# Retention gates and the last two heads' values as a second seven-product block product

## The chip, the cores and the metric

One core of a Trainium2 chip runs the whole program. Its engines work side by side: TensorE (PE in the profile, with its weight loads as PEld), VectorE (DVE), ScalarE (ACT), GpSimd (POOL) and the queues that issue transfers (SP for plain loads, POOL for loads that add to what is already there). The metric is device time in microseconds (us) of one execution, as the median of several runs.

## The reference

A trunk of two layers over 512 tokens of width 1024, in float32. Cut to what matters here:

```python
y = rms_norm(h, mix_norm[i])
proj = y @ w_in[i]                     # [512, 1024] @ [1024, 6144]
x_lru, g_lru, q, k, v, g_ret, u_sgu, v_sgu, g_sgu = jnp.split(proj, split_points, axis=-1)
lru_out = rg_lru(causal_depthwise_conv(x_lru, ...), ...)
ret_out = retention(q, k, v, positions, ret_norm[i])   # 6 heads of 128, chunks of 128 tokens
sgu_out = spatial_gating(u_sgu, v_sgu, ...)
mixed = jnp.concatenate([lru_out * silu(g_lru), ret_out * silu(g_ret), sgu_out * silu(g_sgu)], -1)
h = h + mixed @ w_out[i]
z = rms_norm(h, ple_norm[i])
h = h + sigmoid(z @ w_ple_gate[i]) * (p[i] @ w_ple_proj[i])
```

In retention a head's output rows `o` (per token) are normalised, `o * rsqrt(mean(o*o) + EPS) * g_norm`, and then multiplied by the gate. The widths are 768 for q, k, v and g_ret (6 heads of 128) and 512 for v_sgu.

## The kernel before, in words

Activations lie as feature rows: a tile has 128 features on the partitions and 512 tokens along them. Every float32 operand of a large product is split in a high and a low part, and a product takes three matmuls, high·high, high·low, low·high (`mm3`, lines 212 to 216). A feature step (`feat_steps`) makes 128 output features for all 512 tokens: 8 blocks of the inner dimension times 3 matmuls of 512 columns, 24 in all.

Weights come in chunks of 128 x 1024 (`plan`, the list of all chunks in the order of use). `emit_raw` loads a chunk, `emit_cv` splits it: ACT casts it to `whi` (line 165) and DVE subtracts to get `wlo` (line 170). For a few chunks (`xl` features 3 to 5, without the first layer's feature 3) ACT writes the negated cast and POOL's queue adds the stored weights to it (lines 167 and 168). `prefetch` runs `LOOK` = 4 chunks ahead of use; `whi`, `wlo` and `raw` have four buffers each.

V of the SGU and the values of heads 0 to 3 are token rows (tokens on the partitions), 512 columns each. They are made by a block product with seven multiplications in place of eight (`FAST`, Strassen's scheme in Winograd's form): the tokens, the inner dimension and the columns are halved, four operands on the token side are sums (`fast_sums`, tiles `uy`), and the weight-side sums are made by the load itself, by adding stored quarter blocks in the tile `rawq` (`W11`, then `Ta`, `Tc`, `Td` each on top of the last) or in `raw` (`Tb`, two blocks). Each of the seven steps (`fast_step`) takes two chunks and 2 x 4 x 3 = 24 matmuls of 512 columns. Lines 609 to 623 add the products up in `v4` and `vs`. The values of heads 4 and 5 come from `tok_steps`, two steps of 48 matmuls of 256 columns ahead of head 4. The gate of a head is a feature step (`gr`), scaled by the norm row `R` and put through Silu on ACT (`silu_scaled`).

The order of a layer: six conv-channel steps `xl`, the seven products, layer norm (`ln_apply`), then SGU steps (`gs`, `u`) with the LRU groups (`lru_group`, four groups of two blocks of 96) between them, SGU's output product (`sgu_out`), the six heads, six LRU gate steps `gl`, the output products `oret` and `olru`, and the gated embedding. A head has the feature steps k, q and gr; then its small matmuls hang between later steps by a countdown: `side.extend([[1, scores], [2, states], [3, omm], [5, otr]])`, where `step` counts down by one behind its matmuls. `scores` takes transposes and products of k and q, `states` the chunk states, `omm` the outputs with their mean square and rsqrt, `otr` the transposes back to feature rows and the product with the gate, which is then split (`split_to`) for `oret`. k, q, rope's halves (`rt`) and the square of the outputs (`oq`) lie in tiles with one buffer each, `rt` and `oq` in the same one (`qt`). Background work waits in two lists (`bg`, three items a step, and `lazy`, one a step), such as the splits of the LRU operands (`lru_split`, tiles `xc`), the gates' tanh, exp and sqrt, and the rope tables.

The program order sets only the priority. A planner puts the instructions on the engines in its own order of readiness, so an instruction can run long before its place in the text if its inputs and buffers are there.

Of the kernel before, what the change touches and what calls it, by code (L numbers as in the profile page):

```python
# [30 lines left out]
FIRST = ("W11", "W21", "Ta")  # L31
RSQRT_MAGIC = 1597463007.0
# [35 lines left out]
def blocks_of(chunk):  # L68

    l, kind, idx, n = chunk  # L70
    if kind != "fast":
        return [chunk]
    return [(l, "quad", (q, idx[1]), n) for q in {"Ta": ("W12",), "Tc": ("W22",), "Tb": ("W12", "W22"), "Td": ("W21",)}.get(idx[0], idx[:1])]
# [6 lines left out]
def rows(chunk):  # L80
# [4 lines left out]
SLOTS = [  # L85
    {"y": range(0, 16), "uy": range(16, 32), "v": range(36, 40), "vs": range(32, 36), "xc": range(16, 20), "sgu": range(22, 30), "v45": (30, 31),
     "ret": list(range(22, 30)) + list(range(32, 36)), "lru": list(range(36, 40)) + list(range(16, 22)) + [30, 31], "p": range(32, 36)},
    {"y": range(16, 32), "uy": range(0, 16), "v": range(36, 40), "vs": range(32, 36), "xc": range(0, 4), "sgu": range(6, 14), "v45": (14, 15),
     "ret": list(range(6, 14)) + list(range(32, 36)), "lru": list(range(36, 40)) + list(range(0, 6)) + [14, 15], "p": range(0, 4)},
    {"y": range(0, 0)},  # L90
]
# [3 lines left out]
def trunk(ctx, tc, a):  # L95
# [30 lines left out]
    def after(i):  # L126

        l, kind, idx, n = chunks[i]
        before = {"Ta": "W11", "Tc": "Ta", "Td": "Tc"}.get(idx[0]) if kind == "fast" else None
        return chunks.index((l, kind, (before, idx[1]), n)) if before else -1  # L130

    def emit_raw():
# [18 lines left out]
    def emit_cv():  # L151
# [9 lines left out]
        else:  # L161
# [4 lines left out]
            if kind == "in" and 3 * P <= idx < OFF["gl"] and i > 3:  # L166
# [63 lines left out]
    first3 = [wp.tile([P, 1024], F32, tag="raw", name=f"raw{i}") for i in range(3)]  # L230
# [75 lines left out]
    def norm_stat(t0=0, nt=4, diag=True):  # L306
# [21 lines left out]
        nrm["dg"] = [tp.tile([P, S], F32R, tag=t, name="n" + t, bufs=b) for t, b in (("sgm", 1), ("sq", 2))]  # L328
# [17 lines left out]
    def feat_steps(l, y, kinds, evicts, look=LOOK, n_bg=3, mid=None, n_lazy=1, tag=()):  # L346
# [3 lines left out]
        def pe():  # L350
# [3 lines left out]
            for k in range(KD):  # L354
                for acc, (wh, wl) in zip(accs, ws):
# [5 lines left out]

    def tok_steps(l, y, off, evict):

        ws = []
        for th in range(2):
            accs = []

            def pe():
                if not ws:
                    ws.extend([take(l, "inv", (off, 0)), take(l, "inv", (off, 1))])  # L370
                acc = bank(shape=(P, 2, 256))
                accs.append(acc)
                for j in range(2):
                    t = slice(P * (2 * th + j), P * (2 * th + j) + P)
                    for k in range(KD):
                        wh, wl = ws[k // 4]
                        c = slice(256 * (k % 4), 256 * (k % 4) + 256)
                        mm3(acc[:, j, :], y[k][0][:, t], y[k][1][:, t], wh[:, c], wl[:, c], k == 0, k == KD - 1)

            step(pe, lambda: evict(th, accs[0]), look=LOOK if th == 0 else LOOK - 2)  # L380
# [25 lines left out]
    def rope_tables():  # L406
        ang, n1, n2, tmp = slot_tiles((20, 21, 30, 31), "rope")
# [20 lines left out]
        def last():  # L428
            V.tensor_scalar(ang, ang, float(np.float32(3.1415925)), -float(np.float32(3.1415925)), op0=ALU.min, op1=ALU.max)
            SC.activation(sinT, ang, AF.Sin, scale=inv[:, 1:2])  # L430
            SC.activation(n1, ang, AF.Abs)
            SC.activation(cosT, n1, AF.Sin, scale=-1.0, bias=cst[:, 0:1])

        ops = [first, rnd(n1, big), red(n1, c1[0]), red(n1, c1[1])]
        ops += [red(n1, c1[2], out=tmp), red(n1, c1[3], out=tmp, x=tmp), rnd(n2, 2 * np.pi, x=tmp), red(n2, c2[0])]
# [51 lines left out]
    for l in range(DEPTH):  # L487
# [101 lines left out]
        banks = {}  # L589

        def fast_step(name, xn, at):

            first = name in FIRST

            def pe():
                ws = [take(l, "fast", (name, c)) for c in range(2)]
# [9 lines left out]
            def ev():  # L606
                for t in range(2):
                    acc = banks[at][t]
                    if name == "W11":
                        SC.copy(v4[t], acc)  # L610
                    elif name == "W21":
                        V.tensor_add(v4[t], acc, v4[t])
                    elif name == "Tc":
                        SC.copy(vs[t], acc)
                    elif name == "Tb":
                        SC.copy(vs[2 + t], acc)
                        V.tensor_sub(vs[2 + t], banks["Y"][t], vs[2 + t])
                        ln_stats(2 + t)
                    elif name == "W22":
                        V.tensor_sub(vs[t], acc, vs[t])  # L620
                        ln_stats(t)
                    elif name == "Td":
                        SC.copy(v4[2 + t], acc)
# [78 lines left out]
        for product in FAST:  # L702
            fast_step(*product)
        ln_apply()
# [352 lines left out]
```

## Time and profile before

| | |
|---|---|
| median of 3 runs | 924.42 us (923.02 to 926.29) |
| profiled execution, its own time | 922.63 us |
| its span, first to last instruction | 920.9 us |
| mean granted TensorE clock | 0.995 |
| PE matmuls busy | 900.2 us, 4354 instructions |
| DVE busy | 663.6 us, 1284 instructions |
| ACT busy | 459.8 us, 665 instructions |
| POOL busy | 48.8 us, 49 instructions |

Busy time of PE is modelled from pipelined matmuls: a matmul shows 0.39 us although the next one starts sooner, so the rate is read from the distance of two starts. A row of the stage view lists, after the stretch and its length, busy time and (instructions) of PE, PEld, DVE, ACT and POOL, the granted clock, the share of the transfer engines and GB/s; instructions that only touch the edge of a stretch are counted in it. A row of the timeline has start and length in us, engine, line, operation, tile written <- tiles read, and in brackets the idle time before and what ended it.

### The profile page before, as it was taken

The page shows a single profiled execution, that of the slowest core. Times are in us where ns is not written, and L with a number is a line of the kernel's source. Part 1 is how long each engine was busy: PE and PEld are TensorE (multiplying, and loading weights), DVE is VectorE, ACT ScalarE, POOL GpSimd, SP SyncE. Part 2 cuts the span into 40 slices and gives each one's busy share as a digit, 9 for nine tenths or more (in the row PEclk, how much of TensorE's full clock was granted, in tenths as well). Part 3 has the DMA queues.
Part 4 walks back from the last instruction along what each step waited for, and adds up shares of the span by engine and source line. Part 5 has one row for each costly group of instructions (what it writes and reads, how often), then busy time and mean ns, then how long its engine had stood idle before and what let it go on. Part 6 is the DMA issues. An engine that isn't in the chain of part 4 may idle for free.

```text
span 920.9 us, 11714 instructions
## 1 busy us (share of the span) xinstructions
PE 900.2 (98%) x4354; PEld 752.0 (82%) x4354; DVE 663.6 (72%) x1284; ACT 459.8 (50%) x665; POOL 48.8 (5%) x49
## 2 busy tenths in 40 slices
PE   9999998999999999999998999899999999999997
PEld 7788786788898888888887888688889888888886
DVE  7899997978766764448737998788776676534564
ACT  6655769823332433335537556976233334334353
POOL 0210000000000000200211000000000000011020
PEclk9999999999999999999999999999999999999999
DMA  8976222332222332331257852132221223333302
GB/s 298 247 177 224 59 92 70 115 115 75 87 69 98 99 109 95 126 137 69 92 128 147 215 164 75 52 125 97 77 92 69 95 82 109 88 106 128 102 1 92
DMA packets 34745, 103.57 MB, mean 112 GB/s; under 512 B 4608, under 2 KB 5632, under 8 KB 34688
## 3 DMA queue, kind: packets, MB, share of 16 engines
q1 hardware_dynamic: 27680, 85.42, 27.8%
q0 software_dynamic: 3024, 11.01, 6.5%
q10 hardware_dynamic: 3984, 6.38, 2.4%
q8 instruction: 34, 0.56, 0.2%
q14 instruction: 23, 0.19, 0.1%
HBM read 94.41 MB, written 2.10 MB: 105 GB/s over the span
## 4 chain that ended last, share of the span: by engine, by line
PE 82%; DVE 9%; DMA 3%; issue 3%; ACT 2%; SPq 0%; DVEq 0%; POOL 0%; ACTq 0%; POOLq 0%
PE acc L216 24%; PE acc L215 24%; PE acc L214 24%; DVE wlo L170 2%; DMA rawq<-in_wall 1%; PE sc L826 1%; PE o L849 1%; DMA wlo<-in_wall 1%; PE o L851 1%; PE kv L837 1%; PE pp L214 1%; DVE xcv L551 1%; PE pp L216 1%; PE pp L215 1%; DVE rope L415 1%
## 5 line engine op out<-in xcount | busy, mean ns | idle before, releaser
L165 ACT CAST whi<-raw 128x1024 fp32r<-128x1024 f32 (+2 forms) x157 | 153.1, 978 | 306.4 <-PE acc L215 217.0
L216 PE MATMUL acc<-y,wlo 128*128 128x512 f32 x608 | 238.9, 393 | 4.6 <-DMA wlo<-in_wall 4.6
L214 PE MATMUL acc<-y,whi 128*128 128x512 f32 x608 | 242.6, 399 | 0.3 <-DVE whi L470 0.2
L215 PE MATMUL acc<-y,whi 128*128 128x512 f32 x608 | 238.1, 392 | 0.0
L170 DVE TENSOR_TENSOR wlo<-raw,whi 128x1024 fp32r<-128x1024 f32 (+2 forms) x152 | 171.2, 1129 | 75.5 <-ACT whi L165 75.4
L216 PEld LDWEIGHTS acc<-y,wlo 128*128 128x128 f32 x608 | 114.5, 188 | 29.9 <-DMA wlo<-in_wall 5.5
L214 PEld LDWEIGHTS acc<-y,whi 128*128 128x128 f32 x608 | 115.0, 189 | 24.0 <-ACT rg L663 0.6
L215 PEld LDWEIGHTS acc<-y,whi 128*128 128x128 f32 x608 | 114.9, 189 | 22.9 <-DVE y L284 0.4
L304 POOL TENSOR_TENSOR nacc<-nacc,sq 128x512 f32<-128x512 f32 (+1 forms) x21 | 28.6, 1360 | 497.4 <-ACT sq L294 497.4
L214 PE MATMUL acc<-z,whi 128*128 128x512 f32 (+1 forms) x144 | 53.0, 368 | 0.0
L216 PE MATMUL acc<-z,wlo 128*128 128x512 f32 (+1 forms) x144 | 52.8, 367 | 0.0
L215 PE MATMUL acc<-z,whi 128*128 128x512 f32 (+1 forms) x144 | 52.8, 367 | 0.0
L216 PE MATMUL acc<-ml,wlo 128*128 128x512 f32 x96 | 37.4, 390 | 0.0
L215 PE MATMUL acc<-rm,whi 128*128 128x512 f32 x96 | 37.4, 390 | 0.0
L214 PE MATMUL acc<-ml,whi 128*128 128x512 f32 x96 | 37.4, 390 | 0.0
L215 PE MATMUL acc<-ml,whi 128*128 128x512 f32 x96 | 37.4, 390 | 0.0
L214 PE MATMUL acc<-rm,whi 128*128 128x512 f32 x96 | 37.4, 390 | 0.0
L216 PE MATMUL acc<-rm,wlo 128*128 128x512 f32 x96 | 37.4, 390 | 0.0
L214 PE MATMUL acc<-whi,y 128*128 128x256 f32 (+1 forms) x112 | 37.2, 332 | 0.0
L215 PE MATMUL acc<-wlo,y 128*128 128x256 f32 (+1 forms) x112 | 36.9, 329 | 0.0
L216 PE MATMUL acc<-whi,y 128*128 128x256 f32 (+1 forms) x112 | 36.8, 329 | 0.0
L914 DVE TENSOR_TENSOR hT<-hT,acc 128x512 f32<-128x512 f32 x16 | 11.0, 687 | 29.9 <-PE acc L216 29.9
(233 smaller groups left out, 1651.9 us busy)
## 6 DMA issues: line engine op xcount, KB each, us to landing
raw<-in_wall SPq DMA_DIRECT2D x119, 512.0 KB, 3.4
raw<-in_wall SPq DMA_DIRECT2D x32, 384.0 KB, 3.0
rawq<-in_wall POOLq DMA_DIRECT2D x12, 512.0 KB, 6.5
wlo<-in_wall POOLq DMA_DIRECT2D x5, 512.0 KB, 9.0
hT<-in_xT SPq DMA_DIRECT2D x8, 256.0 KB, 5.9
rawq<-in_wall SPq DMA_DIRECT2D x4, 512.0 KB, 6.2
raw<-in_wall POOLq DMA_DIRECT2D x4, 512.0 KB, 9.7
out_dram<-o SPq DMA_DIRECT2D x8, 256.0 KB, 2.1
```

The source lines that it names most:

```text
L165: SC.copy(hi[:m, :n], r[:m, :n])
L170: V.tensor_sub(lo[:m, :n], r[:m, :n], f32(hi[:m, :n]))
L214: T.matmul(out, wh, xh, start=first, stop=False, skip_group_check=more)
L215: T.matmul(out, wh, xl, start=False, stop=False, skip_group_check=more)
L216: T.matmul(out, wl, xh, start=False, stop=last, skip_group_check=more)
L304: (V if d == KD - 1 else e).tensor_add(nrm["acc"][:, c], nrm["acc"][:, c], sq[:, :n])
L415: return lambda: V.scalar_tensor_tensor(out, n, -c, x, op0=ALU.mult, op1=ALU.add)
L551: V.scalar_tensor_tensor(u[:, j:], xs[:, : S - j], col(V_CW, l * 24 + 6 * (3 - j) + c), u[:, j:], op0=ALU.mult, op1=ALU.add)
L826: T.matmul(b[:, n, :], k[:, c], q[:, c], start=True, stop=True)
L837: T.matmul(kv[:, n, :], hd["kn"][:, n, :], values(h, n), start=True, stop=True)
L849: T.matmul(o[:, c], hd["s"][:, n, :], values(h, n), start=True, stop=n == 0)
L914: V.tensor_add(hT[:, d, :], hT[:, d, :], accs[j])
```

## The change

The gates of all six heads (768 columns) and the values of heads 4 and 5 (256 columns) become a second block product of seven steps on the same token sums, with 2 x 512 columns. Its results are token rows `d1` and `d2`, so the gate is multiplied into the normalised output rows before the transposes back. The `gr` steps and `tok_steps` go. A head has two feature steps; the countdown of the small matmuls runs in half steps. The split of q and k weights takes the road by ACT and POOL, that of `xl` the one by DVE. `raw` has three buffers in place of four; the LRU operands use the tile `rawq`; `lru_split` moves ahead in the background list; layer norm runs behind the first of the new products; some slots and tags move.

```diff
+FAST_COLS = (((OFF["v"], 512),), ((OFF["vs"], 512),)), (((OFF["gr"], 512),), ((OFF["gr"] + 512, 256), (OFF["v"] + 512, 256)))
...
-        out += [(l, "fast", (name, c), 1024) for name, _, _ in FAST for c in range(2)]
+        out += [(l, "fast", (name, c, g), 1024) for g in range(2) for name, _, _ in FAST for c in range(2)]
...
-            if h == 4:
-                out += [(l, "inv", (OFF["v"] + P * h, kh), 1024) for kh in range(2)]
-            out += [(l, "in", OFF[n] + P * h, 1024) for n in ("k", "q", "gr")]
+            out += [(l, "in", OFF[n] + P * h, 1024) for n in ("k", "q")]
...
+        "d1": [40, 41, *at(12, 13)], "d2": at(4, 5, 8, 9), "sgu": at(2, 3, 6, 7, 10, 11, 14, 15),
...
-            r = wp.tile([P, 1024], F32, tag="raw", name=f"raw{i}")
+            r = wp.tile([P, 1024], F32, tag="raw", name=f"raw{i}", bufs=3)
...
-            if kind == "in" and 3 * P <= idx < OFF["gl"] and i > 3:
+            if kind == "in" and OFF["q"] <= idx < OFF["v"]:
...
-    def step(pe, evict=None, look=LOOK, n_bg=3, pre=None, n_lazy=1):
-        prefetch(st["use"] + look)
-        pe()
+    passed = []
+
+    def half_step():
+
+        passed.append(1)
         for e in side:
             e[0] -= 1
         while side and side[0][0] <= 0:
             side.pop(0)[1]()
+
+    def step(pe, evict=None, look=LOOK, n_bg=3, pre=None, n_lazy=1):
+        prefetch(st["use"] + look)
+        passed.clear()
+        pe()
+        half_step()
+        if not passed[1:]:
+            half_step()
...
             for k in range(KD):
+                if k == KD // 2 and len(kinds) == 1:
+                    half_step()
...
-                for b, x in zip(LRU_GROUPS[g], act_tiles(SLOTS[l]["xc"], f"xc{l}{g}_")):
+                for b in LRU_GROUPS[g]:
+                    t = wp.tile([P, 2 * S], F32R, tag="rawq", name=f"xc{b}", bufs=2)
+                    x = t[:, :S], t[:, S:]
...
-        def fast_step(name, xn, at):
+        def fast_step(g, name, xn, at):
 
             first = name in FIRST
+            r1, r2 = ((v4, vs), (d1, d2))[g]
...
-            fast_step(*product)
-        ln_apply()
+            fast_step(0, *product)
+        bg.append(ln_apply)
+        for product in FAST:
+            fast_step(1, *product)
+        drain()
+
+        def gates(t):
+
+            def f():
+                for x in (d1[t], d2[t][:, :256]):
+                    SC.activation(x, x, AF.Silu, scale=rn[:, t : t + 1])
+
+            return f
+
+        bg.extend([gates(t) for t in range(4)])
...
-                bg.append(lru_split(c - 1))
+                (bg.append if c == 2 else bg.appendleft)(lru_split(c - 1))
...
-                    bg.append(lru_split(3))
+                    bg.appendleft(lru_split(3))
...
-            if h == 4:
-                v45 = slot_tiles(SLOTS[l]["v45"], f"v45{l}_")
-                tok_steps(l, y, OFF["v"] + P * h, lambda th, acc: SC.copy(v45[th].rearrange("p (a b) -> p a b", a=2), acc))
...
-                    SC.activation(ob[:, P * t : P * t + P], o[:, P * t : P * t + P], AF.Copy, scale=r[:, t : t + 1])
+                    c = slice(P * t, P * t + P)
+                    V.scalar_tensor_tensor(ob[:, c], o[:, c], r[:, t : t + 1], gate(h, t), op0=ALU.mult, op1=ALU.mult)
...
-                oT = bank("o", 1, name="oT")
+                oT = bank(name="oT")
...
-                V.scalar_tensor_tensor(m, oT, col(V_RN, l * 6 + h), hd["sg"], op0=ALU.mult, op1=ALU.mult)
-                split_to(rm[h], m)
-
-            feat_steps(l, y, [("in", OFF["gr"] + P * h)], [g_ev])
-            side.extend([[1, scores], [2, states], [3, omm], [5, otr]])
+                w = col(V_RN, l * 6 + h)
+                SC.activation(rm[h][0], oT, AF.Copy, scale=w)
+                V.scalar_tensor_tensor(rm[h][1], oT, w, f32(rm[h][0]), op0=ALU.mult, op1=ALU.subtract)
+
+            side.extend([[2, scores], [3, states], [4, omm], [7, otr]])
```

## Rows read from the trace of the kernel before

**Rows 1.** The page's first part: busy us, share of the span, instructions.
```profile
PE 900.2 (98%) x4354; PEld 752.0 (82%) x4354; DVE 663.6 (72%) x1284; ACT 459.8 (50%) x665; POOL 48.8 (5%) x49
```

**Rows 2.** Stage view: layer 0's SGU, single stretches, a retention head.
```profile
30.59:45.49 14.90, 12.79 (x49) 10.09 (x48) 12.74 (x28) 10.20 (x17) 4.04 (x5) 0.89 1.04 222
482.35:496.02 13.67, 11.19 (x50) 8.94 (x48) 8.83 (x22) 7.56 (x13) 2.42 (x3) 1.00 1.06 223
133.53:148.86 15.33, 12.50 (x50) 9.38 (x49) 15.21 (x22) 15.21 (x20) 0.00 (x0) 0.89 0.14 46
583.28:597.74 14.46, 11.44 (x50) 8.12 (x49) 13.77 (x20) 13.65 (x17) 0.00 (x0) 1.00 0.13 46
248.36:254.19 5.83, 5.83 (x52) 5.83 (x51) 4.64 (x16) 0.70 (x2) 0.00 (x0) 1.00 0.27 90
214.40:234.72 20.32, 20.32 (x110) 17.33 (x109) 15.96 (x40) 6.75 (x14) 0.00 (x0) 1.00 0.23 79
...
96.00:142.00 46.00, 42.22 (x201) 34.26 (x199) 45.55 (x78) 35.75 (x46) 0.00 (x0) 1.00 0.22 69
142.00:172.00 30.00, 29.82 (x123) 23.37 (x124) 24.60 (x34) 26.66 (x35) 0.00 (x0) 0.94 0.22 73
```

**Rows 3.** PE's waits: line waited for, us in total, times, longest.
```profile
PE acc L214 <- ACT xc L495: 5.1, 2, 2.8
PE acc L216 <- DMA wlo<-in_wall: 4.6, 2, 2.5
...
PE mx L716 <- DVE vs L636: 1.0, 1, 1.0
```

**Rows 4.** Timeline of PE in a feature step, twelve matmuls apart.
```profile
180.41 0.39 PE L214 MATMUL acc<-y,whi 128*128 128x512 f32 x1
...
183.13 0.39 PE L214 MATMUL acc<-y,whi 128*128 128x512 f32 x1
```

**Rows 5.** Groups by line: count | busy us, mean ns | idle before.
```profile
L165 ACT CAST whi<-raw 128x1024 fp32r<-128x1024 f32 (+2 forms) x157 | 153.1, 978 | 306.4 <-PE acc L215 217.0 <-issue 68.2 <-PE acc L216 16.4
...
L170 DVE TENSOR_TENSOR wlo<-rawq,whi 128x1024 fp32r<-128x1024 f32 x16 | 19.5, 1221 | 1.9 <-ACT whi L165 1.8
...
L830 DVE SCALAR_TENSOR_TENSOR s<-sc,kf,mask 128x128 f32<-128x128 f32 x48 | 13.5, 345 | 1.4 <-PE sc L826 1.2
...
L167 ACT ACTIVATE wlo<-raw 128x1024 fp32r<-128x1024 f32 x5 | 5.3, 1052 | 0.0
```

**Rows 6.** Landing of `rawq` loads at 499 and at 30 us; the page's plain loads.
```profile
DMA to landing us min/median/max: 5.1/5.3/7.7
...
DMA to landing us min/median/max: 7.3/7.8/8.3
...
raw<-in_wall SPq DMA_DIRECT2D x119, 512.0 KB, 3.4
```

**Rows 7.** Timeline of DVE, and one row of PE, around a head's outputs.
```profile
220.16 0.69 DVE L798 TENSOR_TENSOR rtq<-acc,sinT 64x512 f32<-64x512 f32 x1 [0.85 <-PE acc L216]
...
228.00 0.48 PE L214 MATMUL acc<-y,whi 128*128 128x512 f32 x1
...
228.76 0.68 DVE L800 TENSOR_TENSOR q<-acc,cosT 128x512 f32<-128x512 f32 x1
...
230.91 0.69 DVE L858 TENSOR_REDUCE ov<-oq 128x4 f32<-128x512 f32 x1 [0.75 <-ACT oq L856]
...
234.02 0.16 DVE L862 TENSOR_TENSOR rs_y<-rs_y,of 128x4 f32<-128x4 f32 x1
```

**Rows 8.** Timelines of DVE and POOL at 30 and at 480 us.
```profile
30.63 1.39 DVE L854 TENSOR_TENSOR of<-of 128x4 f32<-128x4 f32 x1
...
31.03 0.96 POOL L577 TENSOR_SCALAR_AFFINE_SELECT ws<-ws 128x512 f32<-128x512 f32 x1
...
480.64 1.22 DVE L170 TENSOR_TENSOR wlo<-rawq,whi 128x1024 fp32r<-128x1024 f32 x1
...
480.65 0.87 POOL L145 DMA_DIRECT2D raw<-in_wall  x1 [1.49 <-DMA raw<-in_wall]
```

More of the change, by code (lines that the diff above doesn't have):

```diff
@@ L72, in blocks_of @@
         return [chunk]
-    return [(l, "quad", (q, idx[1]), n) for q in {"Ta": ("W12",), "Tc": ("W22",), "Tb": ("W12", "W22"), "Td": ("W21",)}.get(idx[0], idx[:1])]
+    return [(l, "quad", (q, *idx[1:]), n) for q in {"Ta": ("W12",), "Tc": ("W22",), "Tb": ("W12", "W22"), "Td": ("W21",)}.get(idx[0], idx[:1])]
 def stored():
@@ L81, in rows, with slots, at @@
     return LB if chunk[1] == "lg" else P
[L85 to L91, printed above, removed]
+def slots(y0, z0):
+    def at(*offs):
+        return [z0 + o for o in offs]
+    return {
+        "y": range(y0, y0 + 16), "uy": range(z0, z0 + 16), "vs": range(32, 36), "v": range(36, 40),
+        "d1": [40, 41, *at(12, 13)], "d2": at(4, 5, 8, 9), "sgu": at(2, 3, 6, 7, 10, 11, 14, 15),
+        "ret": [*at(2, 3, 6, 7, 10, 11, 14, 15), *range(32, 36)],
+        "lru": [*at(0, 1), *range(36, 40), *at(12, 13, 4, 5, 8, 9)], "p": [40, 41, 42, 32],
+    }
+SLOTS = [slots(0, 16), slots(16, 0), {"y": range(0, 0)}]
 @with_exitstack
@@ L129, in after @@
         before = {"Ta": "W11", "Tc": "Ta", "Td": "Tc"}.get(idx[0]) if kind == "fast" else None
-        return chunks.index((l, kind, (before, idx[1]), n)) if before else -1
+        return chunks.index((l, kind, (before, *idx[1:]), n)) if before else -1
     def emit_raw():
@@ L228, in trunk @@
     hT = cp.tile([P, KD, S], F32, name="hT")
-    first3 = [wp.tile([P, 1024], F32, tag="raw", name=f"raw{i}") for i in range(3)]
+    first3 = [wp.tile([P, 1024], F32, tag="raw", name=f"raw{i}", bufs=3) for i in range(3)]
     half = [slice(0, 512), slice(512, 1024)]
@@ L327, in norm_stat @@
         V.tensor_sub(rl, r, f32(rh))
-        nrm["dg"] = [tp.tile([P, S], F32R, tag=t, name="n" + t, bufs=b) for t, b in (("sgm", 1), ("sq", 2))]
+        nrm["dg"] = [tp.tile([P, S], F32R, tag=t, name="n" + t, bufs=b) for t, b in (("m2", 2), ("sq", 2))]
         for x, dg in zip((rh, rl), nrm["dg"]):
@@ L360, in feat_steps @@
         step(pe, lambda: [e(acc) for e, acc in zip(evicts, accs)], look=look, n_bg=n_bg, n_lazy=n_lazy)
[L362 to L380, printed above, removed]
     def split_to(x, src, e=None):
@@ L406, in rope_tables @@
     def rope_tables():
-        ang, n1, n2, tmp = slot_tiles((20, 21, 30, 31), "rope")
+        (ang,), n1, n2 = slot_tiles((42,), "ang"), cosT, sinT
         big = 2 * np.pi * 2.0**14
@@ L589, in trunk @@
         banks = {}
-        def fast_step(name, xn, at):
+        d1 = slot_tiles(SLOTS[l]["d1"], f"d1{l}_")
+        d2 = slot_tiles(SLOTS[l]["d2"], f"d2{l}_")
+        def fast_step(g, name, xn, at):
             first = name in FIRST
+            r1, r2 = ((v4, vs), (d1, d2))[g]
             def pe():
-                ws = [take(l, "fast", (name, c)) for c in range(2)]
+                ws = [take(l, "fast", (name, c, g)) for c in range(2)]
                 if first:
@@ L783, in values, with gate @@
         def values(h, n):
-            if h < 4:
-                return v4[n][:, P * h : P * h + P]
-            return v45[n // 2].rearrange("p (a b) -> p a b", a=2)[:, n % 2, P * (h % 2) : P * (h % 2) + P]
+            return v4[n][:, P * h : P * h + P] if h < 4 else d2[n][:, P * h - 256 : P * h - 128]
+        def gate(h, n):
+            return d1[n][:, P * h : P * h + P] if h < 4 else d2[n][:, P * h - 512 : P * h - 384]
         for h in range(NH):
-            if h == 4:
-                v45 = slot_tiles(SLOTS[l]["v45"], f"v45{l}_")
-                tok_steps(l, y, OFF["v"] + P * h, lambda th, acc: SC.copy(v45[th].rearrange("p (a b) -> p a b", a=2), acc))
+            hd = {}
             hd = {}
@@ L994, in layout @@
         if kind == "quad":
[L995 to L996 removed]
+            k, cols = int(idx[0][1]) - 1, FAST_COLS[idx[2]][int(idx[0][2]) - 1]
+            x = np.stack([np.concatenate([w_in[l][P * j : P * j + P, f0 : f0 + nf] for f0, nf in cols], 1) for j in (4 * idx[1] + k, 4 * idx[1] + 2 + k)], 1)
         elif kind == "p":
```

31 lines of the change are left out of this document (12 added, 19 removed).

## The prediction

> **What bounds the kernel now.** I read the page's engine lines first [rows 1]: PE is busy nearly all of the span. A busy PE only counts if it is at its rate, so I read the spacing next [rows 4]: twelve matmuls apart, two starts of 512 columns lie 2.72 us apart, 0.2267 us each; the granted clock of such stretches is 1.00, the 2.4 GHz level (the head in [rows 2]). A step of 24 matmuls is 24 × 0.2267 = 5.44 us. Where PE keeps this spacing it is the bound, and only its matmul count and its waits set the time. So I looked for stretches with the count right and the time too long [rows 2, 3]. There are three kinds. The two conv-channel steps `xl4`, `xl5` take 14.90 us in layer 0 and 13.67 in layer 1 for 48 matmuls (10.88): 4.0 and 2.8 us lost, to `wlo` from the accumulating DMA [rows 3]; in layer 0 the clock's mean fell to 0.89 there. The last SGU gate step, LRU group 2 and the first SGU output matmuls (24 + 12 + 10 = 46 matmuls, 10.43 us) take 15.33 and 14.46: 4.9 and 4.0 us lost, behind the LRU operand copies `xc` of ACT [rows 3]. And 1.0 us goes to the layer norm's `vs`. In the retention heads nothing is lost: a head's cycle of 20.32 us is PE throughout, DVE 15.96 [rows 2]. DVE is the second bound in layer 0's SGU stage, with 45.55 of 46 us, and LRU groups 2 and 3 are hard on ACT (26.66 of 30).
>
> **The change part by part.**
>
> *Matmuls.* Twelve `gr` feature steps go: 12 × 5.44 = 65.3 us. The four half-steps of `tok_steps` go: one half is 48 matmuls of 256 columns in 5.83 us [rows 2], four are 23.3 us. Fourteen product steps come, each 2 × 4 × 3 = 24 matmuls of 512 columns like the products there now: 14 × 5.44 = 76.2 us. Sum: **-12.4 us**. All three lie on PE, at its rate, so this part is as sure as the spacing.
>
> *Weight splits.* `gr` and `v45` had 16 chunks in all, the second product has 28. A chunk costs ACT a cast of 0.98 us and DVE a subtraction of 1.22 [rows 5]. The 24 `k` and `q` chunks leave DVE for a second ACT pass of 1.05 us and an accumulating DMA on POOL. In retention that takes three subtractions (3.66 us) and two 512-column operations (the R multiply and one of the split, 2 × 0.69, priced by the 0.68 of the q multiply [rows 7]) off DVE, and adds four gate multiplies of 128 columns at 0.345 [rows 5], 1.38: 15.96 - 3.66 - 1.38 + 1.38 = 12.3 us of DVE per head, under PE's 20.32 - 5.44 - 0.1 = 14.8. The second product needs 14 × 1.22 + 6 × 0.68 = 21.2 us of DVE in 38.1 us of PE, so DVE gets some 17 us there in which rope tables and layer norm can run that now crowd the SGU stage. The eight gate activations per layer sit on ACT, 35.75 of 46 us busy there [rows 2]; each is shorter than the cast of 0.98, so at most 7.8 of the 10.2 us free. All this costs nothing while PE covers it. It loads 16 blocks of 512 KB a layer, 8.4 MB in 38 us or 220 GB/s, which is the rate of the crowded stretch at 30.59 (222, the transfer engines' share 1.04); hence the crowded landing times below.
>
> *The `xl` chunks go back to DVE.* The wait for their DMA goes, at most 6.8 us. But DVE then has two more subtractions: in layer 0, 12.74 + 2.4 = 15.1 us of work where PE will need only 10.88, so it is 4 us behind and the next thing late is `Ta`, whose sums and weight split DVE makes. I keep 1.0 of the 4.0. In layer 1 it has 8.83 + 2.4 = 11.2 against 10.88, about even; I keep 1.9 of the 2.8. **-2.9 us** (0 to -6.8).
>
> *Layer norm a product earlier:* the wait on `vs` goes, **-1.0** (0 to -1.0).
>
> *`lru_split` to the front of the background list.* Now the copies for group 2 stand behind tanh, exp and sqrt of group 1; ACT is busy 15.21 of 15.33 us there, so the order decides. Ahead of them, the copy is ready a whole gate step (5.44) before PE asks. Of 8.9 us I take **-5.0**, near the middle between all (-8.9) and the little (-2) that is left if the sigmoids then come late, since ACT's work is the same and PSUM waits on it.
>
> *New waits.* The sums in `rawq` are a chain: split, accumulate, split. Let t = 0 be the start of the first product's last step, where `W11` of the second gets weight buffers (four pairs, two per step). Cast 1.05, subtraction 1.22, landing 5.3 alone or 7.8 crowded [rows 6], cast, subtraction: 9.8 to 12.3 us; `Ta` needs it at two steps, 10.88. So up to 1.5 us late, 4 with DVE two subtractions behind too. I take 0.8 a layer, **+1.6** (0 to +8). `raw` with three buffers: the second `Tb` chunk must wait for a `W21` chunk's split, then load (3.4), accumulate, split: 1.05 + 1.22 + 3.4 + 5.3 to 7.8 + 2.27 = 13.2 to 15.7 us of the 16.3 that three steps leave; **+0.5** for four places (0 to +4). The first `k` chunk: 2 × 1.05 + 5.3 to 7.8 = 7.4 to 9.9 us, against two output steps and LRU group 3 (13.6); ACT is 26.66 of 30 busy and may start it late: **+0.5** (0 to +3). Behind each such wait PE's queue stands still; DVE and ACT catch up.
>
> *The heads' chain.* Scores now come one step after q instead of two, and states and outputs half a step apart. Count from the end of a head's outputs, the earliest at which q may be overwritten (one buffer). Now: the step behind the outputs starts at 228.00; the q multiply starts at 228.76, the square's sum at 230.91, the rsqrt chain ends at 234.2 [rows 7]. With one more operation of 0.7 q is done 2.2 us after the outputs, and it is needed after a k step, 5.44: 3 us of cover. The normalised rows are ready after 6.2 plus four gate multiplies, 7.6; the transposes stand behind 36 matmuls of 512 columns at least, 8.2. So PE stays the bound, on the second count by little; I take 0.1 a head for handovers, **+1.2** (0, since nothing is lost now, to +29, below).
>
> *POOL.* 24 + 16 - 5 = 35 accumulating DMAs more, 0.87 us each on an idle engine [rows 8]. Does POOL disturb DVE? Once it does: an `of` multiply of four columns, 0.16 elsewhere [rows 7], takes 1.39 beside POOL's mask of `ws`, and both end within 0.03 us of each other. But beside a DMA issue the weight subtraction keeps its 1.22. The Trainium skill, page "SBUF — State Buffer", section "Who interferes with whom", says that the two share a port pair as an exclusive lock, by which the loser of a collision stands still for the other's whole instruction, and that DVE in two-port modes can starve descriptor generation. The first pair of rows agrees with a lock; the second shows none for a DMA issue beside this subtraction. By the row the 24 issues in the heads cost nothing.
>
> *Sum:* -12.4 - 2.9 - 1.0 - 5.0 + 1.6 + 0.5 + 0.5 + 1.2 = **-17.5 us**. The profiled execution took 922.63 (span 920.9 and 1.7 around it), so 905.1; the median of the runs shown is 1.8 above it, so I state 924.4 - 17.5 = 906.9, **907 us**.
>
> **The rivals.**
>
> *Waits move into the second product.* `Ta` and `Tb` are late at their upper ends (+12 instead of +2.1): 917. For it: the crowded landing and DVE's fullness in layer 0. Against: the later links of the same chain lose nearly nothing in the first product, and DVE has slack in the second.
>
> *ACT stays the bound at the LRU groups*, so that 2 of the 8.9 come back, and nothing of the 6.8: 907 + 3.0 + 2.9 = 913. For it: ACT full there, and gate and `k` passes added. Against: the lost time is one late copy, not the sum of ACT's work.
>
> *The heads become a DVE latency chain: slower.* `qt` is one buffer for rope's halves and for the square of the outputs. If in DVE's order the norm chain takes it first, q's rope starts after the gate multiplies: 0.8 for the square, 3.3 from its sum to the rsqrt (230.91 to 234.2), 1.4, and then four operations, 2.7: 8.2 us, where scores want it at 5.44 and the transposes of k, some tenths. That is about 2.4 us a head, +29 in all and -1.2 for what the sum has there: 935. It decides from 17.5 / 12 = 1.5 us a head. For it: the outputs now come in the step of q itself. Against: the planner orders by readiness (the `of` multiply of a head's outputs runs at 30.63, in layer 0's first steps [rows 8]), and q's halves are ready a block of outputs before the square; the half at 220.16 ran as soon as its step's last matmul released it [rows 7].
>
> *A port lock between POOL and DVE in the heads.* Two issues of 0.87 a head stop DVE: 12.3 + 1.7 = 14.0 of 14.8 us. By the sum PE still covers it; my estimate is half a microsecond a head lost to order, 913. The page named above would have it so for two-port operations; the second pair of rows 8 speaks against.
>
> **How the numbers follow.** My forecast 0.62; waits in the second product 0.18; ACT 0.06; the heads' chain 0.10; the lock 0.04. Less than 0.3% (2.8 us, about what the three runs' spread of 3.3 allows) is no change. All cases but the third end faster, with some of the second's tail near no change; the heads' chain at half its price is no change too. Faster 0.86, same 0.05, slower 0.09. Low end: the matmuls and all three recoveries without any new wait, -12.4 - 6.8 - 1.0 - 8.9 = -29.1, would be 895; 896 leaves hardly anything out. High end: the second product's and ACT's cases together give 923; 921 leaves about one in ten above, the heads' case.
>
> **What would show it.** PE with 4354 - 288 - 192 + 336 = 4210 matmuls; a head's cycle of 14.8 us; no wait of PE on the accumulated `wlo` in the `xl` steps; DVE not full in the second product; `xc` no longer ended by ACT at group 2. Wrong would be: PE gaps at the second `Ta` or at `Tb` above 2 us, a cycle above 16 us with PE waiting for q, or the 46 matmuls around LRU group 2 still at 14 us.

## The result and the profile after

The changed kernel takes 931.56 us (median of 4 runs, 930.40 to 932.75), the kernel before 925.05 beside it (4 runs, 923.02 to 926.29): ratio 1.0076, 95% interval 1.0057 to 1.0095, so slower by 6.5 us where 17.5 faster was forecast. The profiled execution of the changed kernel took 930.40 (span 928.5).

The page's first part (busy us, share of the span, instructions of each engine), to be read beside [rows 1]:

```profile
PE 894.8 (96%) x4210; PEld 739.4 (80%) x4210; DVE 654.5 (70%) x1313; ACT 482.4 (52%) x662; POOL 79.6 (9%) x84
```

The 4210 matmuls are there, and PE's busy time fell by 5.4 us; but the span grew by 7.6, so PE now stands still for longer. PE's waits (line waited for, us in total, times, longest), to be read beside [rows 3]:

```profile
PE acc L230 <- ACT vs L619: 7.8, 2, 5.7
PE acc L230 <- ACT xc L495: 4.6, 2, 2.3
PE acc L230 <- ACT whi L171: 3.7, 3, 3.1
...
PE acc L230 <- ACT vs L617: 2.6, 3, 1.2
PE sc L838 <- DVE q L816: 2.4, 2, 1.2
```

Two waits of before are gone (the accumulated `wlo` and the layer norm's `vs`), `xc` has hardly moved, and the accumulator copies of the products (L617, L619) and their weight casts (L171) are new. The stage view says where (columns as in [rows 2]): `xl3` to the first product, layer 0's two products (the two rows part where the last step of the first one, `W22`, starts; that product ends at 91.08), the same in layer 1 (parted between the products), the matmuls around LRU group 2 in both layers, one head:

```profile
24.38:41.45 17.07, 17.07 (x77) 13.91 (x76) 16.93 (x53) 7.27 (x11) 4.32 (x5) 1.00 0.91 213
...
41.45:86.32 44.87, 37.55 (x150) 28.92 (x149) 39.32 (x71) 25.02 (x34) 4.34 (x5) 0.92 0.66 170
86.32:133.95 47.63, 44.33 (x191) 35.26 (x189) 36.24 (x70) 28.98 (x39) 6.31 (x7) 1.00 0.76 174
...
497.30:541.84 44.54, 41.07 (x169) 32.46 (x168) 38.81 (x59) 21.86 (x29) 6.98 (x8) 0.96 0.78 192
541.84:586.00 44.16, 40.27 (x170) 32.63 (x169) 27.57 (x52) 25.29 (x34) 4.37 (x5) 0.96 0.71 169
...
181.16:195.14 13.98, 11.15 (x49) 8.19 (x48) 13.29 (x20) 13.86 (x18) 0.00 (x0) 1.00 0.16 48
633.21:647.98 14.77, 12.48 (x49) 9.35 (x48) 14.08 (x20) 14.63 (x19) 0.00 (x0) 0.88 0.15 46
...
259.42:274.33 14.91, 14.91 (x86) 12.82 (x85) 11.71 (x38) 6.00 (x10) 1.73 (x2) 1.00 0.64 140
```

The conv steps lose nothing now (PE is busy in all of the 17.07 us), and a head takes 14.91 us with PE busy throughout. The products are where the time went. At 0.2268 us a matmul (and 0.46 for the bias rows) layer 0's two should need 76.7 us and take 92.5. The spacing of the starts, taken matmul by matmul, parts the 15.8 us lost into 11.0 in the first product and 4.8 in the second; in layer 1, 6.4 and 6.1. Measured in the same way, the one product before the change lost 2.4 us in both layers together. So some 26 us came new, and they turn a gain into a loss.

How the worst gap comes about, from three timelines of the changed kernel (start, duration, instruction, idle before and its releaser): POOL, ACT, PE in layer 0's first product.

```profile
58.49 0.86 POOL L151 DMA_DIRECT2D raw<-in_wall  x1 [7.87 <-DMA raw<-in_wall]
59.10 1.14 POOL L151 DMA_DIRECT2D rawq<-in_wall  x1
...
64.77 1.04 ACT L171 CAST whi<-raw 128x1024 fp32r<-128x1024 f32 x1 [3.21 <-DMA raw<-in_wall]
...
70.60 1.05 ACT L171 CAST whi<-rawq 128x1024 fp32r<-128x1024 f32 x1 [1.17 <-DMA rawq<-in_wall]
...
74.96 0.81 ACT L549 ACTIVATE xcv<-xs,vec 128x512 f32<-128x512 f32 x1 [2.59 <-DMA U<-xcv]
75.68 1.03 ACT L171 CAST whi<-raw 128x1024 fp32r<-128x1024 f32 x1
...
77.56 0.57 ACT L619 COPY vs<-acc 128x512 f32<-128x512 f32 x1
...
72.15 0.39 PE L232 MATMUL acc<-whi,uy 128*128 128x512 f32 x1
78.19 0.80 PE L230 MATMUL acc<-whi,y 128*128 128x512 f32 x1 [5.65 <-ACT vs L619]
```

Read it upwards. PE waits for the copy of `Tb`'s accumulator. The copy stands in ACT's queue behind two casts and a conv tap that waits 2.59 us for a store of the tile that it writes. Before that ACT had stood 3.21 us for the second `Tb` chunk (64.77) and twice more for the `Td` sums. That chunk's accumulate stood 7.87 us at the head of POOL's queue until its plain load had landed, and the `Td` sums queue behind it at 59.10. The rows show this order, not what each link costs; that takes the runs. They show that the gap has two causes, neither of which makes it alone: when the early table operations go (run 3), PE no longer stops in front of `Td` (its longest stop in that product is then 2.37 us between two starts, within `Tb`), although that accumulate still goes out only at 54.77 us; and without `Tb`'s accumulates (run 4) 2.36 us are left of the 6.04 between the two starts.

### The profile page after: what moved, and what is told of

It reads as the page before. It is cut to its first block, busy times and chain, and to the rows that moved or that the text cites. A ratio compares the mean times of both kernels' runs of the same rounds, so it can differ in the third digit from the quotient of the medians.

```text
span 928.5 us, 11542 instructions
## 1 busy us (share of the span) xinstructions
PE 894.8 (96%) x4210; PEld 739.4 (80%) x4210; DVE 654.5 (70%) x1313; ACT 482.4 (52%) x662; POOL 79.6 (9%) x84
## 4 chain that ended last, share of the span: by engine, by line
PE 78%; DMA 7%; DVE 6%; ACT 6%; issue 2%; POOL 0%; ACTq 0%; DVEq 0%; POOLq 0%
PE acc L230 23%; PE acc L231 23%; PE acc L232 23%; DMA rawq<-in_wall 3%; DMA raw<-in_wall 2%; DMA U<-xcv 1%; DVE wlo L176 1%; ACT whi L171 1%; PE sc L838 1%; PE o L861 1%; PE kv L849 1%; PE o L863 1%; PE pp L230 1%; PE pp L232 1%; PE pp L231 1%
## 5 line engine op out<-in xcount | busy, mean ns | idle before, releaser
L171 ACT CAST whi<-raw 128x1024 fp32r<-128x1024 f32 (+2 forms) x153 | 148.6, 975 | 269.4 <-PE acc L231 202.4
L176 DVE TENSOR_TENSOR wlo<-raw,whi 128x1024 fp32r<-128x1024 f32 (+2 forms) x129 | 143.8, 1115 | 91.0 <-ACT whi L171 90.9
L230 PE MATMUL acc<-y,whi 128*128 128x512 f32 x512 | 204.5, 399 | 0.2 <-ACT y L299 0.2
L232 PE MATMUL acc<-y,wlo 128*128 128x512 f32 x512 | 200.5, 392 | 0.0
L231 PE MATMUL acc<-y,whi 128*128 128x512 f32 x512 | 200.0, 391 | 0.0
L230 PEld LDWEIGHTS acc<-y,whi 128*128 128x128 f32 x512 | 96.5, 188 | 19.5 <-ACT y L299 0.7
L231 PEld LDWEIGHTS acc<-y,whi 128*128 128x128 f32 x512 | 96.6, 189 | 19.0 <-DVE y L300 0.2
L171 ACT CAST whi<-rawq 128x1024 fp32r<-128x1024 f32 x32 | 33.6, 1050 | 53.3 <-DMA rawq<-in_wall 24.3
L230 PE MATMUL acc<-whi,uy 128*128 128x512 f32 x128 | 51.9, 408 | 7.6 <-ACT whi L171 3.7
L176 DVE TENSOR_TENSOR wlo<-rawq,whi 128x1024 fp32r<-128x1024 f32 x32 | 39.1, 1224 | 22.3 <-ACT whi L171 22.3
L231 PE MATMUL acc<-wlo,uy 128*128 128x512 f32 x128 | 50.9, 399 | 2.3 <-DVE wlo L176 2.3
L232 PE MATMUL acc<-whi,uy 128*128 128x512 f32 x128 | 50.3, 396 | 0.0
L230 PE MATMUL acc<-whi,y 128*128 128x512 f32 x96 | 38.9, 407 | 7.8 <-ACT vs L619 7.8
L231 PE MATMUL acc<-wlo,y 128*128 128x512 f32 x96 | 38.9, 406 | 0.3 <-DVE wlo L176 0.3
L232 PE MATMUL acc<-whi,y 128*128 128x512 f32 x96 | 38.7, 403 | 0.0
```

Of the source, the lines that this page charges most:

```text
L171: SC.copy(hi[:m, :n], r[:m, :n])
L176: V.tensor_sub(lo[:m, :n], r[:m, :n], f32(hi[:m, :n]))
L230: T.matmul(out, wh, xh, start=first, stop=False, skip_group_check=more)
L231: T.matmul(out, wh, xl, start=False, stop=False, skip_group_check=more)
L232: T.matmul(out, wl, xh, start=False, stop=last, skip_group_check=more)
```

## The experiments

All were run beside the kernel before (923.7 to 924.7 us); the ratios are to it. "Loss" of a product is, as above, the time that its 168 matmuls take beyond the spacing of 0.2268 us.

**1. Room for a fourth raw buffer.** The angle table's tile and one `p` tile move to other slots, and the silu tiles get two buffers (in both places that use them; one is shown):

```
-        (ang,), n1, n2 = slot_tiles((42,), "ang"), cosT, sinT
+        (ang,), n1, n2 = slot_tiles((SLOTS[0]["uy"][0],), "ang"), cosT, sinT
...
-        "lru": [*at(0, 1), *range(36, 40), *at(12, 13, 4, 5, 8, 9)], "p": [40, 41, 42, 32],
+        "lru": [*at(0, 1), *range(36, 40), *at(12, 13, 4, 5, 8, 9)], "p": [40, 41, 32, 33],
...
-        x = tp.tile([P, S], F32, tag="sg", name=f"sx{name}", bufs=3)
+        x = tp.tile([P, S], F32, tag="sg", name=f"sx{name}", bufs=2)
```

> Only makes room: the rotary angles and one ple tile move to slots that are free at that time, the silu tiles have two buffers instead of three; the raw chunks keep three buffers. Every theory: the time of the changed kernel, 931.6, within 2 us; a difference here has to be taken off the next run.

923.70 us, ratio 1.0000 (0.9987 to 1.0012): 7.9 us under the changed kernel. Every theory was wrong here. Layer 0's first product lost 2.7 us instead of 11.0; experiment 3 takes apart what had moved.

**2. Four raw buffers** in that room: `tag="raw", ... bufs=4`.

> The raw chunks have four buffers again, as in the kernel before, in the room made above; all else is the changed kernel. Theory A (late buffer): in the first product the second Tb chunk's plain load waits for the third buffer, its accumulate stands at the head of POOL's queue for it, and the Tc and Td sums queue behind: the first product's 16 us of lost matmul time falls to the 2.4 of before, total 915 to 919, and the second product keeps its 11 us. Rival B (the sums themselves, 24 accumulates and their casts in ScalarE's order, are too slow whatever the buffers): under 4 us gained, 928 to 932. Rival C (the sum tiles that the split conv now shares are the late buffer): no change, 931.

918.22 us, ratio 0.9938 (0.9918 to 0.9958). Against run 1 this is 5.5 us, the buffer alone. The gain lies in layer 1. There the products lose 4.8 and 9.1 us in run 1 and 0.4 and 4.9 here, while in layer 0 they lose 2.7 and 4.0 there and 2.0 and 5.2 here. Layer 1's first product shows how: POOL's second `Tb` accumulate and ACT's cast of that chunk in run 1, and then POOL's two `Tb` accumulates in this run, in which ACT casts both chunks without a wait.

```profile
503.76 0.86 POOL L151 DMA_DIRECT2D raw<-in_wall  x1 [9.66 <-DMA U<-xcv]
...
511.31 1.04 ACT L171 CAST whi<-raw 128x1024 fp32r<-128x1024 f32 x1 [3.62 <-DMA raw<-in_wall]
```

```profile
476.67 0.86 POOL L151 DMA_DIRECT2D raw<-in_wall  x1 [0.21 <-issue]
478.81 0.86 POOL L151 DMA_DIRECT2D raw<-in_wall  x1 [1.28 <-DMA raw<-in_wall]
```

Theory A's mechanism holds there; of the 14 us it was to bring, the larger part came with run 1, in layer 0. Four buffers beside the early tables were not run.

**3. The angle tile alone** (the first line of the diff of run 1).

> The changed kernel with one line different: the tile of the rotary angles lies in a tile of the token sums, which is free only after the second product's last step, instead of in a slot of its own that is free from the start. Theory J (the free slot let the planner run 14 of the angle table's VectorE operations at 18.8 to 34.7 us, ahead of the token sums and weight subtractions of layer 0's first product; with the slot taken they run behind the products as in the run that only made room): the whole gain of that run, 923 to 925 against 931.6, all of it in layer 0. Rival K (it was the silu tiles or the ple slots that gained): 930 to 933.

923.02 us, ratio 0.9989 (0.9971 to 1.0006): the whole gain of run 1, 8.5 us. In the changed kernel, DVE's first and last of the 14 early table operations:

```profile
18.82 0.42 DVE L416 CAST ang<-cosT 128x512 f32<-128x512 int32 x1
...
33.98 0.68 DVE L413 SCALAR_TENSOR_TENSOR ang<-cosT,ang 128x512 f32<-128x512 f32 x1
```

and in this run the first one:

```profile
109.26 0.42 DVE L416 CAST ang<-cosT 128x512 f32<-128x512 int32 x1
```

The 14 operations are 8.0 us of DVE, most of it between the weight subtractions, the rsqrt chain and the token sums of the stage in which DVE is busiest (16.93 of 17.07 us above). Before the change the tables lay in tiles of the token sums, which are busy until the product is over, and began at 83 us. The diff gave them a free slot, and the planner, which orders by readiness, used it. Theory J holds: of the 7.6 us between the two spans 6.8 are there when layer 0's products end (127.2 us against 133.95).

**4. `Tb` without its accumulate**, three raw buffers and the early tables kept: `"Tb": ("W12",)`.

> Leaves out the second block of the Tb weights in both products, so Tb is loaded plainly and has no accumulate on POOL (the last values of that factor are of another matrix); raw chunks keep three buffers. Theory A: what costs is the accumulate that waits at the head of POOL's queue, so this gains as much as four buffers or a little more, 912 to 919. Rival B: the remaining 16 sums are as late as they were, under 5 us gained.

912.65 us, ratio 0.9879 (0.9860 to 0.9898), 18.9 under the changed kernel. Without `Tb`'s eight accumulates, and the 512 KB that each of them moves, the products lose 10.9 us in place of 28.3, with everything else of the changed kernel there. Rival B falls.

**5. The accumulator copies on DVE**: `SC.copy(r1[t], acc)` becomes `V.tensor_copy(r1[t], acc)`, and so for the other three.

> The products' accumulator copies (W11, Tc, Tb, Td, two products) run on VectorE instead of ScalarE; three raw buffers. Theory A with its last step, that ScalarE in order holds the copies behind casts of late chunks: PE's waits for those copies (7.8, 2.6 and 1.2 us in the changed kernel) go, but the chunk itself is next in line, so 3 to 8 us gained, 924 to 928. Rival D (the order on ScalarE is the whole cause): 12 us or more gained, under 920. Rival B: PE waits for the casts instead, nothing gained, 930 to 933.

942.16 us, ratio 1.0196 (1.0181 to 1.0212): 10.6 us slower than the changed kernel, outside all three. PE's longest wait is again for an accumulator copy, this time `Tc`'s (L617), on the other engine; DVE's timeline has the reason:

```profile
PE acc L230 <- DVE vs L617: 12.9, 2, 6.6
...
72.55 1.23 DVE L176 TENSOR_TENSOR wlo<-raw,whi 128x1024 fp32r<-128x1024 f32 x1 [3.88 <-ACT whi L171]
...
74.36 0.69 DVE L617 COPY vs<-acc 128x512 f32<-128x512 f32 x1
```

The subtraction of a late chunk stands in DVE's order as the casts do in ACT's. So ACT's order is only the last link: with the copies on either engine, the one that they share with the split of late weights holds them up.

**6. The second product without sums**, four raw buffers: all seven factors are loaded plainly.

> Four raw buffers; leaves out all added blocks of the second product's weights: its seven factors are loaded plainly, each from its first block, through the raw buffers, with no accumulate and no sum buffer (the gates and the last two heads' values are of other matrices; the count of matmuls is the same). Theory G and rival H both: the second product loses under 1 us in each layer, 907 to 910. Rival I (what delays the second product is ScalarE's casts and copies themselves): it still loses over 3 us a layer, 914 to 918.

905.42 us, ratio 0.9800 (0.9767 to 0.9832), 12.8 under run 2 and under both ranges; the second product's loss falls from 10.2 us in both layers together to nothing. Two 38 us stretches of the second product (the first in layer 0):

```profile
86.77:125.00 38.23, 38.23 (x170) 31.68 (x169) 36.59 (x72) 23.49 (x31) 0.00 (x0) 1.00 0.61 198
532.00:570.00 38.00, 38.00 (x170) 31.46 (x169) 23.23 (x36) 22.30 (x29) 0.00 (x0) 1.00 0.54 172
```

PE is busy throughout, at a transfer rate of 198 and 172 GB/s and with all casts, subtractions and copies there. The loss of the second product comes from its accumulates, not from the work of ACT and DVE or the rate. Rival I falls.

**7. The first `gs` step between the two products**, 5.4 us more for the chain of sums:

```
+        feat_steps(l, y, [("in", OFF["gs"])], [g0_ev])
         for product in FAST:
             fast_step(1, *product)
```

> Four raw buffers, and the first gs step (5.4 us of matmuls) goes between the two products instead of behind them. Theory G (the sums of the second product form one chain behind those of the first, since W11 of the second is loaded into the two sum buffers that Td of the first frees, each link a transfer of 5 to 11 us and a cast): 5.4 us more for the chain in each layer take away most of what the second product still loses (about 4.5 us in each layer), 909 to 912. Rival H (late because POOL and the DMA rings are shared by everything in that stretch, not because of the buffers): the loss moves with it, 916 to 920.

918.68 us, ratio 0.9944 (0.9927 to 0.9961): no gain on run 2. The loss moved with the product (5.5 and 7.2 us, nearly all at `Ta`), as rival H had it. POOL's timeline shows what stands in the way of `Ta`, whose two chunks are the `rawq` at 81.68 and at 86.79:

```profile
81.68 0.86 POOL L153 DMA_DIRECT2D rawq<-in_wall  x1 [21.96 <-DVE wlo L178]
84.17 0.86 POOL L153 DMA_DIRECT2D raw<-in_wall  x1 [1.63 <-DMA raw<-in_wall]
86.21 0.86 POOL L153 DMA_DIRECT2D raw<-in_wall  x1 [1.17 <-issue]
86.79 1.18 POOL L153 DMA_DIRECT2D rawq<-in_wall  x1
```

Both accumulates of `Tb`, needed three steps later, stand ahead of `Ta`'s second one, which lands 10.28 us after its issue.

**8. The second product's `Tb` without its accumulate**, four raw buffers, all running sums kept.

> Four raw buffers (the kernel of 918.2 us); leaves out the second block of Tb's weights in the second product alone, so that of the second product's eight accumulates the two of Tb go and the six of the running sums stay (the gates and last heads' values are of other matrices). Theory L (Ta of the second product is late because Tb's accumulates stand in POOL's queue ahead of it and share the transfer engines, 7 to 11 us a landing instead of 5.3): the second product's 10 us of loss falls to under 4, 911 to 913. Theory G (the running sums' own chain through two buffers): the loss stays above 7 us, 915 to 918.

909.74 us, ratio 0.9849 (0.9826 to 0.9872): 8.5 of the 12.8 us of run 6, with the running sums in place. The second product's loss falls from 10.2 us to 4.4, where theory L had it under 4, and the time is 1.3 us under L's range. Theory L holds in the main, and the chain alone (G) explains at most the other 4.

**9. The same bytes without POOL**: both blocks of the second product's `Tb` come as plain loads, and DVE adds them.

```
+            if k and kind == "fast" and idx[0] == "Tb" and idx[2] == 1:
+                adds[i] = wp.tile([P, 1024], F32, tag="raw", name=f"rawb{i}", bufs=4)
+                nc.sync.dma_start(out=adds[i], in_=source(b))
...
+        if i in adds:
+            V.tensor_add(r, r, adds.pop(i))
```

> Four raw buffers (the kernel of 918.2 us); the two blocks of the second product's Tb weights are both loaded plainly, into two raw buffers, and VectorE adds them, so the same bytes move and the whole computation is there, but POOL's queue has no Tb accumulate in the second product. Theory L1 (Tb's accumulates cost by their place in POOL's queue): most of the 8.5 us that leaving out that block gained come here too, 909 to 912. Theory L2 (they cost by the bytes that share the transfer engines with Ta's sums): under 3 us gained, 916 to 918. If the second raw buffer a chunk is missed elsewhere, it is lost again in front of W22 or u.

913.33 us, ratio 0.9882 (0.9857 to 0.9907): 4.9 of the 8.5 us come back with all the bytes moved. The result lies between L1 and L2; the second product loses 6.6 us, between the 10.2 of run 2 and the 4.4 of run 8. Over half of the cost goes with the accumulates, by their place in POOL's queue or by their landing; the rest, 3.6 us, may be the bytes, DVE's two additions a layer or the second raw buffer that a chunk takes, and these runs do not part them. A run with the accumulates issued behind `Ta`'s, which would test the order alone, was not made.

**10. `xl3` to `xl5` as before**, low parts by ACT and an accumulating DMA, four raw buffers.

> Four raw buffers (the kernel of 918.2 us), and the low parts of xl3 to xl5 are made again by ScalarE and an accumulating DMA as in the kernel before; all else as there. If the trace of the changed kernel is read rightly, the wait for that DMA comes back in both layers, 4.0 and 2.8 us: 924 to 926. If VectorE without those two subtractions is early elsewhere (the prediction's 2.9 us net), 920 to 922.

931.40 us, ratio 1.0080 (1.0051 to 1.0109): 13.2 us slower than run 2, over both ranges. The wait is back, 5.3 us of it by name,

```profile
PE acc L232 <- DMA wlo<-in_wall: 5.3, 2, 2.9
```

and the second product loses 4.2 and 2.6 us more than in run 2. Why it does was not followed up.

**11. The conv split ahead of its step**, four raw buffers:

```
+            if c == 3:
+                bg.appendleft(lru_split(2))
             feat_steps(l, y, [("in", OFF["u"] + P * c)], [u_ev], mid=mix)
-            if c > 1:
-                (bg.append if c == 2 else bg.appendleft)(lru_split(c - 1))
+            if c == 2:
+                bg.append(lru_split(1))
```

> Four raw buffers as in the run of 918.2 us, and the conv split of the third group is put in the background list ahead of the u step before it, so that the step takes it first; in the changed kernel it goes to the front only after that step has taken the tanh, exp and sqrt block. Theory E (that order is why the xc wait stayed, 3.5 and 4.3 us lost in the two layers): both stretches before the third group run at 0.23 us a matmul, 6 to 8 us gained, 910 to 912. Rival F (the split waits for something else, its conv data or the two shared sum buffers): under 2 us gained, 916 to 919.

914.44 us, ratio 0.9903 (0.9871 to 0.9935), by the medians 3.8 under run 2; the intervals overlap, so the trace decides. PE's wait for `xc` is gone from its list, and the 46 matmuls around LRU group 2 take 10.64 us in both layers, where run 2 takes 13.98 and 14.78:

```profile
174.70:185.34 10.64, 10.64 (x50) 8.41 (x49) 10.36 (x16) 10.55 (x14) 0.00 (x0) 1.00 0.05 14
618.32:628.96 10.64, 10.64 (x49) 8.41 (x48) 10.35 (x16) 10.55 (x14) 0.00 (x0) 1.00 0.05 14
```

ACT in the changed kernel, and then in this run:

```profile
181.00 1.34 ACT L681 ACTIVATE lT<-rg,sp 96x512 f32<-96x512 f32 x2
...
186.31 1.34 ACT L688 ACTIVATE sT<-lT,cst 96x512 f32<-96x512 f32 x2
...
188.49 1.14 ACT L495 CAST xc<-U 96x512 fp32r<-96x512 f32 x2
```

```profile
174.54 1.15 ACT L495 CAST xc<-U 96x512 fp32r<-96x512 f32 x2
175.58 1.34 ACT L681 ACTIVATE lT<-rg,sp 96x512 f32<-96x512 f32 x2
```

Theory E holds for the order. In its place PE waits 1.6 us for group 2's sigmoids (`rg`), behind the same block of ACT. From the gate step to group 3's first matmul the two layers are 4.7 us shorter than in run 2; the products, which lie ahead of it, lose 1.6 us more than there.

**12. What gained, together.** First with the `gs` step between the products and the first head's scores half a step later:

> Four raw buffers, the split ahead of the u step, the gs step between the products, and the first head's scores and what follows one half step later (its q is 1.5 us late in each layer). If the theories A, E and G hold the gains add up: 918.2 - 7 - 8 - 2.5, some 900 us, range 897 to 906. If E or G falls, 907 to 913.

911.40 us, ratio 0.9857 (0.9824 to 0.9890), in the range for the case that E or G falls; then without the `gs` step:

> The parts that gained, together: four raw buffers, the third group's conv split ahead of the u step, and the first head's scores half a step later; the gs step stays behind the products. From 914.4 with the first two, less the 2.2 us that the first heads lose there: 912, range 910 to 914; under the run with the gs step between the products (911.4) if that move costs something, above it if it gained.

912.52 us, ratio 0.9881 (0.9855 to 0.9908): the step is worth nothing that shows, and PE's wait for the first head's q is gone in both. Last, with run 9's addition in both products:

> The last together with the parts that gained: four raw buffers, VectorE adds Tb's two blocks in both products, the third group's conv split ahead of the u step, the first head's scores half a step later. 912.5 less what the first run of this pair gains on 918.2: by L1 some 904 (902 to 907), by L2 910 to 912.

905.75 us, ratio 0.9795 (0.9776 to 0.9814), in L1's range and under both kernels. That it is near the 907 forecast for the change itself is no support for that sum: it comes by edits that the change does not have. Its first line on the page:

```profile
PE 886.9 (98%) x4210; PEld 734.5 (81%) x4210; DVE 663.1 (73%) x1321; ACT 481.9 (53%) x662; POOL 71.6 (8%) x76
```

## Why the prediction was wrong

*Matmuls, -12.4:* right; 4210 of them, at the spacing of before, and PE at it in the heads.

*`xl` back to DVE, -2.9:* under-sized. All 6.8 us are back, although DVE was as full as I said (16.93 of 17.07 us); run 10 puts the part at 13 us once the second product follows.

*Layer norm, -1.0:* right; the wait is gone.

*`lru_split` to the front, -5.0:* the step failed, from the code. I read "ahead of tanh, exp and sqrt" from the diff; for group 2 the call stands behind the step that has already taken that block. 7.9 of the 8.9 us stayed (13.98 and 14.77 us for 46 matmuls). Put where I thought it was, it makes the stretch up to group 3 4.7 us shorter in both layers together (run 11; 3.8 by the medians): the size was right, the reading of the order was not.

*New waits, +2.1 for `Ta` and `Tb`:* the step that made the sign wrong; 28.3 us of loss in the products against 2.4 before. The rival that priced these waits at 12 us named the right chunks, but neither the size nor the place: it put them in the second product, and 15.1 of the 25.9 us that are new lie in the first. Two of the prediction's own signs of being wrong came in, gaps over 2 us at `Ta` and behind `Tb`, and 46 matmuls around group 2 still at 14 us. Three things were missed.
- The tables. I let "rope tables" fill the slack of the second product, and did not look at when their new tile is free. They ran at 18.8 us, and moving that tile to one of the token sums gave 8.5 us (run 3).
- The third buffer, +0.5 forecast, 5.5 measured with the tables out of the way (run 2). The sum of 13.2 to 15.7 us against 16.3 took the chunk's own chain and left out the accumulates queued behind its waiting one on POOL and the copies queued behind its cast on ACT.
- The second product's sums, +1.6 forecast, 12.8 measured with four raw buffers (run 6), 8.5 of them with `Tb`'s accumulates, which the sum for `Ta` did not have (run 8). I let each chunk of `Ta` have a landing of 5.3 to 7.8 us. In layer 1 its second chunk was issued right behind a `Tb` accumulate and landed 10.25 us later, and ACT stood 5.48 us at its cast:

```profile
539.68 0.86 POOL L151 DMA_DIRECT2D raw<-in_wall  x1 [0.93 <-DMA raw<-in_wall]
540.22 1.22 POOL L151 DMA_DIRECT2D rawq<-in_wall  x1
...
550.83 1.04 ACT L171 CAST whi<-rawq 128x1024 fp32r<-128x1024 f32 x1 [5.48 <-DMA rawq<-in_wall]
```

*First `k` chunk, +0.5:* no wait. *The heads, +1.2:* hardly there; the cycle is 14.91 us, 0.03 over the 20.32 less a step of 5.44, and the slower rival (a DVE chain) did not come. What I had not priced is the first head of each layer, which has no head before it: q comes late, 1.5 us each.

*POOL's port, 0:* nothing against it in the heads, where DVE has 11.71 us of work in 14.91 beside two issues.

The terms as measured in the changed kernel: -12.4 - 6.8 - 1.0 - 1.0 + 25.9 (the products) + 2.9 (first heads) = +7.6, the difference of the two profiled spans (928.5 - 920.9). The 8.5, 5.5 and 12.8 are not summed: they were taken on different kernels, and run 4, which takes 18.9 by one edit, shows that they overlap.

## What to carry to other kernels

A tile that moves to a free slot moves its work too: where a planner orders by readiness, ask of every changed allocation when the tile is now free, and what will run then. A wait is priced with the queue behind it: an accumulating transfer waiting for its plain load holds all later accumulates, the engine that splits the late chunk holds the accumulator copies, and the product waits for those. And "to the front of the list" is worth nothing once the list has been served; read the order off the call, not off the name.

## What the runs showed of the hardware

After some gaps PE restarts slowly. In the changed kernel's products this happens three times: behind 6.04 us between two starts in layer 0 (72.15 to 78.19), behind 2.52 us in layer 1 (526.67 to 529.20), and there again behind 3.52 and 1.26 us (548.41 to 553.19). The stretches are (stage view of the changed kernel; the granted clock is the third column from the right):

```profile
78.19:82.92 4.73, 4.73 (x13) 3.73 (x13) 4.73 (x9) 0.58 (x1) 0.00 (x0) 0.57 0.72 216
82.92:86.32 3.40, 3.40 (x16) 2.81 (x15) 2.67 (x7) 1.05 (x1) 0.86 (x1) 1.00 0.28 86
...
529.20:533.00 3.80, 3.80 (x10) 2.98 (x11) 3.80 (x8) 2.32 (x3) 0.00 (x0) 0.55 0.71 204
...
553.20:557.00 3.80, 3.80 (x10) 2.99 (x11) 3.63 (x11) 1.05 (x2) 0.86 (x1) 0.55 0.55 80
```

The granted clock is 0.57, 0.55 and 0.55, near the 1.2 GHz level, with matmuls 0.43 us apart instead of 0.227, and then 1.00 again. That adds 2.0, 1.7 and 1.7 us to the gaps, 5.4 of the 26 us, which no wait in the list names. PE in the second of them:

```profile
530.08 0.63 PE L232 MATMUL acc<-whi,y 128*128 128x512 f32 x1
530.50 0.63 PE L230 MATMUL acc<-whi,y 128*128 128x512 f32 x1
```

The length of the gap alone does not decide it. PE waits 2.29 us for `xc` at group 2 in both layers; behind it the clock is 1.00 in layer 0 and falls to the lower level in layer 1:

```profile
189.15:193.00 3.85, 3.31 (x13) 2.19 (x14) 3.85 (x6) 3.80 (x5) 0.00 (x0) 1.00 0.13 38
641.20:645.00 3.80, 3.80 (x10) 2.73 (x11) 3.80 (x6) 3.75 (x5) 0.00 (x0) 0.61 0.14 39
```

What does decide it these runs do not show.

The Trainium skill, page "TensorE: Matmul & The Clock Gate", section "Wait — 56ns, not 53.3ns?", gives 426.7 ns from start to start at the lower level for 512 columns; the rows agree. For the upper level it gives 215.7 ns; here it is 226.7 [rows 4], and the sums above go by that.

An accumulating DMA of 512 KB landed in 5.44, 5.66 and 6.36 us where no other was under way (at 553.43, 49.76 and 253.19 us of the changed kernel); of four issued within 4 us at 80.5 us of run 2 the last landed after 11.26, and the longest in the changed kernel took 13.56 (at 513.27), issued behind two others.
